# Part of the second layer's weight subtractions on POOL instead of DVE, in a two-layer transformer kernel

## The chip, the cores and the metric

The kernel runs on one core of a Trainium2 chip. The metric is the device time of one execution, from its start to its end, in microseconds (us). A core has five engines that run side by side, each with its own queue of instructions: TensorE (PE) multiplies matrices, VectorE (DVE) and ScalarE (ACT) work on elements, GpSimd (POOL) does too, and SyncE (SP) here issues the loads of weights. Data lie in SBUF; TensorE writes its sums to PSUM.

## The reference

Two layers over 256 tokens of width 1024, in float32. Each adds a mixer and then a mixture of experts to the residual h:

```python
for layer in range(DEPTH):
    u = rms_norm(h, norm_mix[layer])
    mix = even_mixer(...) if layer % 2 == 0 else odd_mixer(...)
    h = h + mix
    h = h + hierarchical_moe(rms_norm(h, norm_ffn[layer]), ...)
```

The change lies in the odd mixer, the second layer's. It projects u to q, k and v, normalises q and k by heads, rotates them by position (rope), and forms attention with the difference of two softmaxes:

```python
q, k, v = jnp.split(u @ w_in, 3, axis=-1)
q = apply_rope(rms_norm(q.reshape(B_, S_, C_HEADS, 2, C_DH), q_norm), positions)
k = apply_rope(rms_norm(k.reshape(B_, S_, C_HEADS, 2, C_DH), k_norm), positions)
...
o = differential_attention(q, k, v, lam, lambda_init, subln)
return o.reshape(B_, S_, ODD_OUT) @ w_out
```

The mixture of experts has a router and 32 experts with a gate, an up and a down matrix each (w_gate, w_up, w_down), whose 2-MB loads are nearly all that the kernel reads.

## The kernel before

The program runs through the layers in order: even mixer, 32 experts, odd mixer, 32 experts. All weights, those of the mixers (w_mix) and of the experts, pass through one ring of buffers in SBUF; SP issues each load (L112) when the slot that it writes is free, so it runs ahead of the computation by as much as the ring holds.

The products of the mixers are made from two parts of each number. A float32 matrix w is split into hi, which TensorE multiplies fast (type fp32r), and lo = w - hi. `mm3` sums three matmuls per product: hi by hi (L291), hi by lo (L292) and lo by hi (L293). The class `Weights` (L295 to L328) makes these splits: a mixer tile of 2 MB comes in four quarters of 128x1024, for each of which ACT casts hi (L314) and DVE subtracts (L315). `ahead` issues splits while split buffers are free (three pairs, `SPLIT`), `next` hands one out and `done` frees it. `W1` is the second layer's instance, with 32 quarters.

The odd mixer has six such projections (`proj_tok`): four for q and k, two for v, then an output projection (`OutProj`). One projection uses four quarters and 48 matmuls of 512 columns, 24 for each half of the tokens (t = 0 and 1). In the first two quarters the halves alternate, in the last two the first half is finished before the second. Below, quarter 0 to 3 belong to projection 1, 4 to 7 to projection 2, and so on; 24 to 31 to the output projection.

Each half of a q or k projection then goes through `rope`: ACT squares it (L374), DVE sums by heads (L376), ACT makes the factor (L245, L246), DVE scales (L379, L381) and multiplies by the cosines (L846) while POOL multiplies by the sines (L847), and DVE joins both (L848, L849). Then TensorE transposes the heads (L388, four instructions), which `settle` puts behind the matmuls of a later projection. Scores and softmax of the heads (L400, L407 and on) are mixed into the following projections. The square and the rope's results use buffers of one small ring ("s2"), in which a new tile waits for the last reader of the old one.

Which instruction stands where on an engine is set by a scheduler that works through the program with its own estimates. Within an engine the order is then fixed, and instructions wait for each other by semaphores.

Of the kernel before, what the change touches and what calls it, by code (L numbers as in the profile page):

```python
# [8 lines left out]
F32 = mybir.dt.float32  # L9
# [4 lines left out]
ALU = mybir.AluOpType  # L14
# [16 lines left out]
SPLIT = 3  # L31
# [93 lines left out]
def halves(t):  # L125
    return t[:, 0:1024], t[:, 1024:2048]
# [13 lines left out]
def hybrid_kernel(ctx: ExitStack, tc: tile.TileContext, x, pos, vec, wr, wbf, const, rope,  # L140
                  w_mix0, w_mix1, w_gate, w_up, w_down, out):
    nc = tc.nc
    V, A, G, T = nc.vector, nc.scalar, nc.gpsimd, nc.tensor
# [151 lines left out]
    class Weights:  # L295


        def __init__(self, n, pairs):
            self.n, self.free, self.used = n, pairs, 0
            self.ready, self.rest = [], []  # L300

        def ahead(self, most=1000):
            while self.n > 0 and most > 0 and (self.rest or self.free > 0):
                most -= 1
                self.n -= 1
                if not self.rest:
                    w = R.take()
                    k = w.shape[1]
                    self.free -= 1
                    self.rest = list(zip([w[:, :, i * P:i * P + P] if k == KD else w[:, i * k // 2:(i + 1) * k // 2, :]  # L310
                                          for i in range(2)], R.alloc(F32R)))
                w, t = self.rest.pop(0)
                hi, lo = (a.rearrange("p (k f) -> p k f", k=w.shape[1]) for a in halves(t))
                self.split = A.copy(out=hi, in_=w)  # L314
                V.tensor_tensor(out=lo, in0=w, in1=hi.bitcast(F32), op=ALU.subtract)  # L315
                if not self.rest:
                    R.drop(1)
                self.ready.append((hi, lo))
# [1029 lines left out]
            with tc.issue_after(silu[0].ins):  # L1348
                A.preload_act_table_set(SET6)

    W1 = Weights(32, SPLIT)
    moe(0, even())
    moe(1, odd(W1))

# [100 lines left out]
```

## Time and profile before

| | us |
|---|---|
| median of 3 runs | 1191.12 |
| lowest, highest | 1190.52, 1192.5 |
| the profiled execution | 1189.17 |
| its span in the trace | 1187.4 |
| TensorE busy | 995.9 (84%) |
| DVE busy | 348.9 (29%) |
| ACT busy | 296.4 (25%) |
| POOL busy | 51.8 (4%) |

The span runs from the first to the last recorded instruction of the profiled execution. Busy shares are means over stages that differ: the experts fill most of the span, and the odd mixer lies between about 603 and 740 us. In that stretch DVE's and POOL's shares are far higher than in the table. In the rows below names such as w, s, o, pa stand for the program's buffers, "out<-in" for what is written and read, and L-numbers for lines of the kernel before; in the changed kernel lines from the changed place on are higher by one (L315 becomes L316, L388 L389).

### The profile page before, as it was taken

The numbers are of one execution on the slowest core, as the hardware profiler recorded it, in microseconds if no ns is written. First come the engines' busy times: TensorE is split into PE (matmuls) and PEld (weight loads), VectorE is DVE, ScalarE is ACT, GpSimd is POOL, SyncE is SP. The second block draws the span as 40 slices with busy tenths as digits, with TensorE's granted clock in tenths as the row PEclk, the third lists the DMA queues.
The fourth block names the chain that finished last, engine by engine and source line by source line (L and its number), as shares of the span: only waits on it lengthen the run. The fifth ranks groups of instructions, "written<-read, shape, count | busy, mean of one in ns | idle before, by whom it ended". The sixth has DMA issues, their size and how long they took to land.

```text
span 1187.4 us, 17231 instructions
## 1 busy us (share of the span) xinstructions
PE 995.9 (84%) x7284; PEld 589.3 (50%) x7284; DVE 348.9 (29%) x879; ACT 296.4 (25%) x681; POOL 51.8 (4%) x90
## 2 busy tenths in 40 slices
PE   7999998888877877786788999888886868786867
PEld 6878774354433434342356778554452424252523
DVE  6976633011111101010069876211111111110101
ACT  6355623111111111111165475211111111111111
POOL 2020001000000000000002100000000000000000
PEclk9999998989979898889899999899899889889989
DMA  9612999999999999999993349899999999999996
GB/s 376 273 54 83 366 374 428 426 427 426 427 427 426 426 427 427 428 427 428 418 428 160 142 166 361 339 427 427 426 427 426 427 427 426 428 427 427 427 427 276
DMA packets 34882, 442.78 MB, mean 373 GB/s; under 512 B 4080, under 2 KB 4464, under 8 KB 7536
## 3 DMA queue, kind: packets, MB, share of 16 engines
q1 hardware_dynamic: 34800, 441.63, 88.7%
q8 instruction: 59, 0.97, 0.3%
q14 instruction: 23, 0.19, 0.0%
HBM read 440.56 MB, written 1.05 MB: 372 GB/s over the span
## 4 chain that ended last, share of the span: by engine, by line
DMA 49%; PE 41%; DVE 5%; ACT 3%; issue 1%; POOL 0%; SPq 0%; ACTq 0%; DVEq 0%; POOLq 0%
DMA w<-w_up 20%; DMA w<-w_down 15%; DMA w<-w_gate 13%; PE pa L1268 7%; PE pa L293 4%; PE pa L291 4%; PE pa L292 4%; PE pa L1277 4%; PE pb L1094 3%; PE pb L1129 2%; PE pc L1243 2%; PE pb L1196 1%; DVE w L315 1%; PE pa L1243 1%; PE pc L400 1%
## 5 line engine op out<-in xcount | busy, mean ns | idle before, releaser
L1268 PE MATMUL pa<-w,o 128*32 128x512 f32 x1920 | 283.0, 683 | 75.8 <-DMA w<-w_up 68.1
L1268 PEld LDWEIGHTS pa<-w,o 128*32 128x32 f32 x1920 | 70.1, 122 | 253.6 <-issue 156.3
L1277 PE MATMUL pa<-w,hid 128*32 128x256 f32 x1984 | 137.7, 424 | 34.6 <-DVE hid L1132 34.6
L1132 DVE TENSOR_TENSOR hid<-hid,pb 128x128 f32<-128x128 f32 x64 | 18.4, 288 | 474.5 <-ACT hid L1131 474.5
L1126 ACT COPY s<-pa 128x512 f32<-128x512 f32 x68 | 39.9, 586 | 398.7 <-PE pa L1268 358.7
L291 PE MATMUL pa<-w 128*128 128x512 f32 (+1 forms) x320 | 120.1, 377 | 3.3 <-ACT w L314 3.3
L292 PE MATMUL pa<-w 128*128 128x512 f32 (+1 forms) x320 | 119.2, 372 | 1.4 <-DVE w L315 1.4
L293 PE MATMUL pa<-w 128*128 128x512 f32 (+1 forms) x320 | 118.8, 373 | 1.8 <-DVE w L315 1.8
L1129 PEld LDWEIGHTS pb<-ct,s 128*128 128x128 f32 x544 | 66.0, 191 | 103.9 <-ACT s L1126 100.3
L1094 PE MATMUL pb<-s,h 128*128 128x128 f32 x448 | 113.7, 407 | 0.0
L1129 PE MATMUL pb<-ct,s 128*128 128x64 f32 (+1 forms) x544 | 74.2, 280 | 45.4 <-ACT s L1126 45.4
L1094 PEld LDWEIGHTS pb<-s,h 128*128 128x128 f32 x448 | 108.9, 334 | 5.8 <-issue 5.8
L1281 DVE COPY o<-pa 32x256 f32<-32x256 f32 x124 | 52.4, 423 | 200.0 <-ACT o L1281 199.4
L1277 PEld LDWEIGHTS pa<-w,hid 128*32 128x32 f32 x1984 | 63.2, 118 | 82.8 <-DVE hid L1132 41.4
L1281 ACT COPY o<-pa 32x256 f32<-32x256 f32 x124 | 45.0, 363 | 207.2 <-PE pa L1277 177.1
L315 DVE TENSOR_TENSOR w<-w 128x1024 fp32r<-128x1024 f32 x68 | 85.1, 1272 | 10.5 <-ACT w L314 10.3
L314 ACT CAST w<-w 128x1024 fp32r<-128x1024 f32 x68 | 68.6, 1045 | 22.5 <-PE pa L293 17.0
L291 PEld LDWEIGHTS pa<-w 128*128 128x128 f32 x320 | 61.8, 193 | 15.4 <-ACT w L314 4.0
L292 PEld LDWEIGHTS pa<-w 128*128 128x128 f32 x320 | 62.1, 194 | 11.8 <-DVE w L315 1.8
L293 PEld LDWEIGHTS pa<-w 128*128 128x128 f32 x320 | 61.9, 194 | 11.5 <-DVE w L315 2.1
L1113 POOL TENSOR_TENSOR s<-OH,CW 128x128 f32<-128x128 f32 x36 | 14.5, 404 | 901.2 <-PE pb L1129 469.3
L1243 PE MATMUL pc<-o,s 128*128 128x512 f32 (+1 forms) x64 | 38.7, 688 | 11.1 <-DVE o L1281 11.1
(284 smaller groups left out, 754.4 us busy)
## 6 DMA issues: line engine op xcount, KB each, us to landing
w<-w_gate SPq DMA_DIRECT2D x62, 2048.0 KB, 39.1
w<-w_up SPq DMA_DIRECT2D x62, 2048.0 KB, 39.1
w<-w_down SPq DMA_DIRECT2D x62, 2048.0 KB, 39.0
w<-w_mix SPq DMA_DIRECT2D x15, 2048.0 KB, 24.4
w<-w_mix SPq DMA_DIRECT2D x4, 1024.0 KB, 9.9
w<-w_gate SPq DMA_DIRECT2D x4, 1024.0 KB, 35.5
w<-w_up SPq DMA_DIRECT2D x4, 1024.0 KB, 30.7
w<-w_down SPq DMA_DIRECT2D x4, 1024.0 KB, 26.2
```

Source lines behind the costliest of these rows:

```text
L291: T.matmul(out=out, lhsT=lhsT[0], rhs=rhs[0], start=start, stop=False)
L292: T.matmul(out=out, lhsT=lhsT[0], rhs=rhs[1], start=False, stop=False)
L293: return T.matmul(out=out, lhsT=lhsT[1], rhs=rhs[0], start=False, stop=stop)
L314: self.split = A.copy(out=hi, in_=w)
L315: V.tensor_tensor(out=lo, in0=w, in1=hi.bitcast(F32), op=ALU.subtract)
L1094: T.matmul(out=pt[:, k, :], lhsT=hk[:, t, 4 * n + k, :], rhs=og[:, t, :], start=t == 0, stop=t == NT - 1)
L1126: A.copy(out=gs, in_=g.rearrange("p (f k) -> p k f", k=4))
L1129: T.matmul(out=tp[:, k, c], lhsT=gs[:, k, :], rhs=r, start=True, stop=True)
L1243: m = T.matmul(out=y[t][:, n, :], lhsT=Sm[:, t * P:(t + 1) * P], rhs=ys, start=start, stop=stop)
L1268: T.matmul(out=gp[32 * j:32 * j + 32, :], lhsT=xg[:, 4 * (j % 2) + kk, 32 * es:32 * es + 32], rhs=w[j][:, kk, :], start=kk == 0, stop=kk = ...
L1277: m = T.matmul(out=dp[32 * j:32 * j + 32, :], lhsT=hid[:, k, :], rhs=w[k // 2][:, k % 2, 256 * j:256 * j + 256], start=k == 0, stop=k == 3 ...
L1281: (V.tensor_copy if j % 2 else A.copy)(out=ys[32 * es:32 * es + 32, 256 * j:256 * j + 256], in_=dp[32 * j:32 * j + 32, :])
```

## The change

`Weights` gets a flag. For the second layer's weights, when the count of quarters still to come is a multiple of four, the subtraction is issued on POOL (`G`) instead of DVE (`V`). These are quarters 3, 7, 11, ... 31: the last of each projection, and the fourth and eighth of the output projection. The first layer's splits stay as they are.

```diff
--- before.py
+++ after.py
@@ -295,8 +295,8 @@
     class Weights:
 
 
-        def __init__(self, n, pairs):
-            self.n, self.free, self.used = n, pairs, 0
+        def __init__(self, n, pairs, shared=False):
+            self.n, self.free, self.used, self.shared = n, pairs, 0, shared
             self.ready, self.rest = [], []
 
         def ahead(self, most=1000):
@@ -312,7 +312,8 @@
                 w, t = self.rest.pop(0)
                 hi, lo = (a.rearrange("p (k f) -> p k f", k=w.shape[1]) for a in halves(t))
                 self.split = A.copy(out=hi, in_=w)
-                V.tensor_tensor(out=lo, in0=w, in1=hi.bitcast(F32), op=ALU.subtract)
+                E = G if self.shared and self.n % 4 == 0 else V
+                E.tensor_tensor(out=lo, in0=w, in1=hi.bitcast(F32), op=ALU.subtract)
                 if not self.rest:
                     R.drop(1)
                 self.ready.append((hi, lo))
@@ -1348,7 +1349,7 @@
             with tc.issue_after(silu[0].ins):
                 A.preload_act_table_set(SET6)
 
-    W1 = Weights(32, SPLIT)
+    W1 = Weights(32, SPLIT, True)
     moe(0, even())
     moe(1, odd(W1))
```

The scheduler places the instructions anew, on TensorE, DVE, ACT and POOL; SP's order is the same. On POOL, in the odd mixer, the kernel before has these rows behind the expert work (s_4184 and s_4200 are the sine products of projection 1, s_4290 and s_4306 of projection 2, s_4396 and s_4412 of projection 3):

```order
L261 TENSOR_TENSOR w<-s_4048,w 128x4x128
L86 MEMSET w 128x1
L847 TENSOR_TENSOR s_4184<-s_4181,own 128x512
L847 TENSOR_TENSOR s_4200<-s_4197,own 128x512
L847 TENSOR_TENSOR s_4290<-s_4287,own 128x512
L86 MEMSET w 128x1
L847 TENSOR_TENSOR s_4306<-s_4303,own 128x512
L847 TENSOR_TENSOR s_4396<-s_4393,own 128x512
L847 TENSOR_TENSOR s_4412<-s_4409,own 128x512
```

And the changed kernel:

```order
L261 TENSOR_TENSOR w<-s_4048,w 128x4x128
L316 TENSOR_TENSOR w<-w 128x1024 x2
L86 MEMSET w 128x1
L848 TENSOR_TENSOR s_4184<-s_4181,own 128x512
L848 TENSOR_TENSOR s_4200<-s_4197,own 128x512
L316 TENSOR_TENSOR w<-w 128x1024 x2
L848 TENSOR_TENSOR s_4290<-s_4287,own 128x512
L86 MEMSET w 128x1
L848 TENSOR_TENSOR s_4306<-s_4303,own 128x512
L316 TENSOR_TENSOR w<-w 128x1024
L848 TENSOR_TENSOR s_4396<-s_4393,own 128x512
```

Quarters 3 and 7 now stand ahead of the first sine product, quarters 11 and 15 between those of projection 1 and projection 2, and quarter 19 ahead of those of projection 3.

On TensorE, around the transposes of projection 1 (s_4181 and s_4197 are its two halves after rope), the kernel before has:

```order
L292 MATMUL pa<-w 128x512
L293 MATMUL pa<-w 128x512
L388 MATMUL pb<-ct,s_4181 128x128 x4
L291 MATMUL pa<-w 128x512
L292 MATMUL pa<-w 128x512
L293 MATMUL pa<-w 128x512
L291 MATMUL pa<-w 128x512
L292 MATMUL pa<-w 128x512
L388 MATMUL pb<-ct,s_4197 128x128 x4
L293 MATMUL pa<-w 128x512
L291 MATMUL pa<-w 128x512
```

And the changed kernel:

```order
L292 MATMUL pa<-w 128x512
L293 MATMUL pa<-w 128x512
L389 MATMUL pb<-ct,s_4181 128x128 x4
L389 MATMUL pb<-ct,s_4197 128x128 x4
L291 MATMUL pa<-w 128x512
L292 MATMUL pa<-w 128x512
L293 MATMUL pa<-w 128x512
L291 MATMUL pa<-w 128x512
L292 MATMUL pa<-w 128x512
L293 MATMUL pa<-w 128x512
```

The second half's transposes have moved ahead of five matmuls, to stand right behind the first half's. It is the same at projection 2, with three matmuls between them before.

On DVE, around the rope of projection 2 (s_4287 and s_4303 are its halves, sm_4281 and sm_4297 the sums of its squares), the kernel before has:

```order
L381 TENSOR_TENSOR s_4287<-pa,sm_4283 128x512
L846 TENSOR_TENSOR s_4289<-s_4287,own 128x512
L315 TENSOR_TENSOR w<-w 128x1024
L848 TENSOR_TENSOR s_4287<-s_4289,s_4290 128x8x32
L849 TENSOR_TENSOR s_4287<-s_4289,s_4290 128x8x32
L376 TENSOR_REDUCE sm_4297<-s_4295 128x8
L315 TENSOR_TENSOR w<-w 128x1024
L379 TENSOR_SCALAR sm_4299<-sm_4299,rsm 128x8
L381 TENSOR_TENSOR s_4303<-pa,sm_4299 128x512
L846 TENSOR_TENSOR s_4305<-s_4303,own 128x512
L848 TENSOR_TENSOR s_4303<-s_4305,s_4306 128x8x32
L849 TENSOR_TENSOR s_4303<-s_4305,s_4306 128x8x32
```

And the changed kernel:

```order
L382 TENSOR_TENSOR s_4287<-pa,sm_4283 128x512
L847 TENSOR_TENSOR s_4289<-s_4287,own 128x512
L849 TENSOR_TENSOR s_4287<-s_4289,s_4290 128x8x32
L850 TENSOR_TENSOR s_4287<-s_4289,s_4290 128x8x32
L377 TENSOR_REDUCE sm_4297<-s_4295 128x8
L316 TENSOR_TENSOR w<-w 128x1024 x2
L380 TENSOR_SCALAR sm_4299<-sm_4299,rsm 128x8
L382 TENSOR_TENSOR s_4303<-pa,sm_4299 128x512
L847 TENSOR_TENSOR s_4305<-s_4303,own 128x512
L849 TENSOR_TENSOR s_4303<-s_4305,s_4306 128x8x32
L850 TENSOR_TENSOR s_4303<-s_4305,s_4306 128x8x32
```

One subtraction has gone from the first half's rope, between L846 (now L847) and L848 (now L849), and two stand now in front of the second half's scaling where one stood.

## Rows read from the trace of the kernel before

**Rows 1.** The page's fourth part, the chain of work that ended last, by engine.

```profile
DMA 49%; PE 41%; DVE 5%; ACT 3%; issue 1%; POOL 0%; SPq 0%; ACTq 0%; DVEq 0%; POOLq 0%
```

**Rows 2.** The view by windows. First the window in us and its length, then the busy time of each engine with its count of instructions, the granted TensorE clock, the mean busy share of the 16 DMA engines, and GB/s.

```profile
605.00:615.00 10.00, 7.66 (x29) 5.63 (x29) 9.66 (x11) 10.00 (x17) 2.52 (x2) 0.83 1.01 425
...
625.00:635.00 10.00, 9.50 (x44) 7.53 (x43) 9.23 (x12) 5.99 (x9) 3.55 (x2) 1.00 0.92 390
635.00:645.00 10.00, 9.17 (x43) 7.67 (x44) 9.96 (x15) 5.15 (x9) 1.75 (x2) 1.00 0.06 26
645.00:655.00 10.00, 7.79 (x34) 5.08 (x33) 7.99 (x13) 4.93 (x10) 2.67 (x2) 0.83 0.13 25
...
725.00:735.00 10.00, 10.00 (x53) 8.36 (x51) 5.12 (x7) 3.36 (x8) 0.00 (x0) 1.00 0.93 387
...
745.00:760.00 15.00, 13.34 (x99) 9.41 (x102) 2.91 (x12) 4.50 (x11) 0.00 (x0) 0.87 0.65 247
760.00:1000.00 240.00, 198.13 (x1552) 103.14 (x1548) 35.80 (x107) 33.04 (x83) 4.88 (x12) 0.92 1.01 427
```

**Rows 3.** The timeline of SP's queue, which issues the weight loads: start, length, line and operation.

```profile
737.43 0.38 SPq L112 DMA_DIRECT2D w<-w_up  x1
754.30 0.33 SPq L112 DMA_DIRECT2D w<-w_down  x1
```

**Rows 4.** The list of waits from 604 to 660 us, all engines: who waits for whom, us in total, times, longest.

```profile
PE pb L388 <- DVE s L849: 3.5, 2, 2.2
...
DVE s L848 <- POOL s L847: 2.3, 3, 1.2
```

**Rows 5.** The timeline of TensorE (PE) in the same stretch: start, length, line and operation, and in brackets the idle time before it and what ended it.

```profile
617.11 0.38 PE L822 MATMUL pb<-sm,ct 64*128 64x2 f32 x2
...
635.83 0.66 PE L388 MATMUL pb<-ct,s 128*128 128x128 f32 x4 [1.33 <-DVE s L849]
...
637.94 0.39 PE L291 MATMUL pa<-w 128*128 128x512 f32 x1
...
645.87 0.40 PE L293 MATMUL pa<-w 128*128 128x512 f32 x1
...
649.62 0.63 PE L388 MATMUL pb<-ct,s 128*128 128x128 f32 x4 [2.21 <-DVE s L849]
...
650.87 0.79 PE L291 MATMUL pa<-w 128*128 128x512 f32 x1
651.46 0.63 PE L292 MATMUL pa<-w 128*128 128x512 f32 x1
...
653.96 0.40 PE L292 MATMUL pa<-w 128*128 128x512 f32 x1
```

**Rows 6.** The groups of instructions by line from 600 to 756 us: count, busy time, mean ns of one, idle time before.

```profile
L315 DVE TENSOR_TENSOR w<-w 128x1024 fp32r<-128x1024 f32 x32 | 41.7, 1314 | 5.1 <-ACT w L314 5.0
```

**Rows 7.** The timeline of DVE, columns as in rows 5; xN folds N instructions in a row.

```profile
610.25 5.75 DVE L315 TENSOR_TENSOR w<-w 128x1024 fp32r<-128x1024 f32 x5
...
616.00 0.14 DVE L820 TENSOR_TENSOR sm<-vt 64x2 f32<-64x2 f32 x1
...
624.30 0.22 DVE L379 TENSOR_SCALAR sm<-sm,rsm 128x8 f32<-128x8 f32 x1
624.43 1.22 DVE L315 TENSOR_TENSOR w<-w 128x1024 fp32r<-128x1024 f32 x1
...
632.78 2.33 DVE L315 TENSOR_TENSOR w<-w 128x1024 fp32r<-128x1024 f32 x1
...
635.36 0.41 DVE L849 TENSOR_TENSOR s<-s,s 128x256 f32<-128x256 f32 x1
...
641.15 2.32 DVE L315 TENSOR_TENSOR w<-w 128x1024 fp32r<-128x1024 f32 x1
...
649.05 0.42 DVE L849 TENSOR_TENSOR s<-s,s 128x256 f32<-128x256 f32 x1
...
654.58 0.68 DVE L376 TENSOR_REDUCE sm<-s 128x8 f32<-128x512 f32 x1
...
657.80 1.68 DVE L846 TENSOR_TENSOR s<-s,own 128x512 f32<-128x512 f32 x1
```

**Rows 8.** POOL's groups by line and shape over the whole span, columns as in rows 6.

```profile
L1113 POOL TENSOR_TENSOR s<-OH,CW 128x128 f32<-128x128 f32 x36 | 14.5, 404 | 901.2 <-PE pb L1129 469.3 <-DVE CW L1035 179.2 <-issue 135.3
...
L261 POOL TENSOR_TENSOR w<-s,w 128x512 fp32r<-128x512 f32 x4 | 5.1, 1276 | 56.0 <-ACT w L261 56.0
```

**Rows 9.** The timeline of POOL, columns as in rows 5.

```profile
626.39 1.81 POOL L847 TENSOR_TENSOR s<-s,own 128x512 f32<-128x512 f32 x1 [6.31 <-DVE s L381]
632.28 1.74 POOL L847 TENSOR_TENSOR s<-s,own 128x512 f32<-128x512 f32 x1 [4.08 <-DVE s L381]
640.68 1.71 POOL L847 TENSOR_TENSOR s<-s,own 128x512 f32<-128x512 f32 x1 [6.66 <-DVE s L381]
...
654.11 1.70 POOL L847 TENSOR_TENSOR s<-s,own 128x512 f32<-128x512 f32 x1 [5.43 <-DVE s L381]
657.62 1.31 POOL L847 TENSOR_TENSOR s<-s,own 128x512 f32<-128x512 f32 x1 [1.82 <-DVE s L381]
...
678.13 1.28 POOL L847 TENSOR_TENSOR s<-s,own 128x512 f32<-128x512 f32 x1 [2.87 <-DVE s L381]
```

## The prediction

> **What bounds the kernel now.** I read the page first. Its chain of waits is DMA and TensorE by turns, with 5% of it on DVE [rows 1]: whether DVE's subtractions matter must be read from their own stretch. The view by windows shows where that is. From 760 us on the DMA engines are full (share 1.01, 427 GB/s), so the second layer's experts run at the speed of their weights. Of the windows between 605 and 655 us, in the second layer's mixer, four have TensorE at 7.66 to 9.50 of 10 us; DVE is at 9.66 and 9.96 in two of them, and the granted clock at 0.83 in two; by 725 to 735 TensorE is 10.00 of 10 [rows 2]. So the mixer's first half is where DVE holds TensorE, and its second half is bound by TensorE itself.
>
> Does a delay in the mixer reach the end? SP's queue issues an expert's w_up at 737.43 and can issue the next load only at 754.30, when L1216 frees its slot [rows 3]; in 745 to 760 the DMA share is 0.65, about 5 us of idle transfer time [rows 2]. The ring of weights is full by then, so a microsecond lost or won by the mixer moves L1216, the next transfers, and the end by one (a gain by at most those 5 us). I take the factor 1.
>
> What DVE makes TensorE wait for is the rope: the wait list has L388, the transposes of rotated heads, 3.5 us behind DVE's L849 in two waits, and DVE's L848 2.3 us behind POOL's L847 [rows 4]. The two waits are 1.33 and 2.21 us [rows 5]. After the second the matmuls L291 and L292 last 0.79 and 0.63 us, at 653.96 again 0.40: the granted clock is at its lower level (1.2 instead of 2.4 GHz) in between. The work of these 4.34 us (649.62 to 653.96) would take about 2.7 at the usual spacing, so I count 1.6 us for it. The usual spacing is 7.93/35 = 0.227 us a matmul (36 rows from 637.94 to 645.87).
>
> **What one moved subtraction costs.** On DVE the 32 subtractions take 41.7 us, 1314 ns on average [rows 6]; undisturbed it is 1.22 (624.43), spaced by 1.15 where five stand in a row (5.75/5) [rows 7]. POOL does none before, so I bound it. Its two-operand 128x512 takes 1276 ns (L261, fp32r output as here) and 1.28 to 1.31 in the undisturbed L847, its 128x128 404 ns [rows 8, 9]. The slope (1276-404)/384 = 2.27 ns a column gives 1276 + 512x2.27 = 2.44 us for 1024 columns; twice 1.31 is 2.62; if it waits as the slowest L847 does, twice 1.81 is 3.6. I take 2.5 as an estimate, since L261 is nearest.
>
> A page puts it lower: the Trainium skill, "GPSIMD Engine Reference", section 3.1, gives 4497 ns for a two-operand addition of 2048 fp32 elements against 2293 on DVE; half of that is an estimate of 2.25 us, and four subtractions on the path at 0.25 less would bring the sum below to about 1197.5. No run here shows POOL at that length.
>
> Does it run beside DVE? The rows say no, where DVE reads two SBUF operands. L315 at 632.78 takes 2.33 instead of 1.22, and POOL's L847 stands at 632.28 to 634.02; at 641.15 it takes 2.32 against POOL's 640.68 to 642.39; L846 at 657.80 takes 1.68 instead of 0.69 against 657.62 to 658.93 [rows 7, 9]. In each case the DVE instruction ends its normal length after POOL ends. L376 at 654.58 (one operand) lies under POOL's 654.11 to 655.81 and takes its 0.68 [rows 7, 9]. So they take turns by whole instructions, and whichever asks while the other runs is next. A moved subtraction frees 1.15 to 1.22 us of DVE and shuts out every two-operand DVE instruction for 2.5.
>
> The Trainium skill, "SBUF — State Buffer", section "Who interferes with whom", has the same rule: a DVE instruction with two SBUF inputs contends with a GpSimd instruction that reads SBUF, and the holder keeps the shared pair for its whole instruction. The trace agrees (2.33 against 1.22). By the rule the change gives the pair 2.5 us of work for 1.2; without it DVE would simply be 1.2 us shorter, which is the first rival below.
>
> **Part by part.** Eight quarters of 32 go to POOL (3, 7, 11, ... 31). The scheduler also moves their neighbours on TensorE, DVE and ACT; SP keeps its order. I walked the new order with the durations above, from the same state at 610 us. The casts (ACT) and loads stay the same; POOL itself is idle there, so its own 20 us (8x2.5) cost nothing but the port and what is queued behind.
>
> Quarter 3: POOL holds the port about 611.4 to 613.9, where DVE had a run of five subtractions from 610.25 [rows 7]. The small operations behind (L820 at 616.00) end at 617.5, and L822's matmul, now after 25 projection matmuls instead of 29 (at 617.11 before [rows 5]), waits 1.4 us. That uses up most of what the lost subtraction saves DVE.
>
> Quarters 7 and 11, projection 1: the first rope half is ready 1.4 earlier. POOL then has quarter 11 right behind the second half's product, and DVE has quarter 10 between; POOL asks while DVE subtracts, so it is next for 2.5, and L848 and L849 end at about 636.5, not 635.77 (635.36+0.41 [rows 7]). The transposes of both halves now stand together, so 5 matmuls that used the wait before come behind it: 0.7 + 5x0.227 = 1.9 us late.
>
> Quarter 15, projection 2: it stands on POOL in front of the first half's product. From the end of one rope (635.77) to the end of the second half of the next (649.05+0.42 = 649.47 [rows 7]) before took 13.7 us. Now: +0.7 late start, +1.4 since ACT's square waits for the slot that the late rope frees, +2.5 for quarter 15 ahead of the product, -1.15 for its place on DVE, +1.15 since two subtractions instead of one stand in front of the second half: 4.6, that is 654.1. Three matmuls that stood between the halves' transposes come behind (0.7): TensorE is 5.3 late there. This includes the 1.9. Its wait grows from 2.21 to about 5.7.
>
> Quarter 19, projection 3: it shuts out that projection's rope and DVE's work on the first scores. My walk has TensorE wait 2.6 there if the port goes to POOL each time, 1.0 if the score work gets in first: I take the middle, 1.8. Quarter 23: between 0 and 1.0, I take 0.4 (DVE is less full by then). Quarters 27 and 31, of the output projection: TensorE is 10.00 of 10 at 725 to 735 and DVE 5.12 [rows 2], so this slack covers 2.5 us each; without that cover it would be up to 1.3 (2.5-1.2) each.
>
> Sum: 5.3+1.8+0.4 = +7.5. The profiled execution took 1189.17 us (span 1187.4): 1196.7; the median of the runs is 1.95 higher (1191.12), so the forecast is 1198.6, say 1198.5. A second fall of the clock would add 1.6, a port that DVE wins at quarters 15 and 19 would take off about 3.5: its own range is 1194 to 1202.
>
> **Rivals.** *Faster: DVE is relieved.* In 635 to 645 DVE is busy 9.96 of 10, and its L849 is what TensorE waits for. If POOL finds the port while DVE works on PSUM or one-operand instructions, two subtractions less before the second rope of projection 2 (2x1.2 = 2.4) cover its wait of 2.21, one less covers 1.33, and the slow clock's 1.6 goes too: -5.1, 1186.0. It decides if the rope of projection 2 ends before TensorE comes to its transposes, about 646.5. Against it: the free stretches there are of 0.2 to 0.7 us (L376 0.68, L379 0.22), and POOL wants 2.5. Chance 0.17.
>
> *No difference.* The waits change places (1.4 at L822 for 1.33 at L388, quarter 15 within the existing 2.21) and the sum of the TensorE waits stays. It needs quarter 15 not to come ahead of the product. 1191, within 2.4 either way. Chance 0.13.
>
> *Worse than forecast.* No slack anywhere in six projections: 8x(2.5-1.2) = 10.4 and two more falls of the clock at 1.6: +13.6, 1204.7. For it: ropes or scores are tied to DVE in all projections. Against it: full TensorE by 655 to 735. Chance 0.13.
>
> That the change does not do what it says is excluded by the order of the new kernel: eight subtractions stand on POOL.
>
> The Trainium skill, "Perfetto Trace Analysis", section "Optimizing Scalar/DVE Operations", warns that moving work between GPSIMD and DVE might not help since they share a read port. It speaks for the forecast's side, by the rows on L315 above.
>
> **How the numbers follow.** The forecast has 0.57. A measurement of this kernel can tell 0.2%, 2.4 us, from no change. Slower by more than that: 0.57+0.13 = 0.70; same 0.13; faster 0.17. The 80% range leaves out half of the faster case below and a little of the worst above: 1188 to 1204.5.
>
> **What would show it.** Right: eight POOL subtractions of 2.4 to 2.6 us where nobody disturbs them; DVE's two-operand rows of 2.5 to 3.7 us under them; a wait of L389 (the old L388) behind L850 that grows from 2.21 to 5 or 6 us; TensorE at 10 of 10 after 680, and 745 to 760 as before but later by the same amount as the end. Wrong: a POOL row below 1.9 us; DVE rows at 1.2 under POOL's; L389 without waits; or an end that moves less than L1216 does.

## The result and the profile after

The changed kernel takes 1201.37 us, median of 4 runs (1200.39 to 1203.02), against 1190.82 of the kernel before in runs on the same chip (1190.31 to 1192.5): 10.55 us slower, ratio 1.0088 with a 95% interval of 1.007 to 1.0105. The profiled execution took 1203.02 us (span 1201.4), so it stands 1.65 above its median, as that of before stood about as much below. The spans differ by 14.0 us; 1.13 of that lies ahead of the odd mixer, whose first projection matmul starts at 608.17 instead of 607.04. Times below are compared after taking off these 1.13.

The chain that ended last, by engine (the page's fourth part), where [rows 1] stood before, and POOL's new group from the groups by line and shape:

```profile
DMA 51%; PE 35%; DVE 7%; ACT 4%; issue 2%; POOL 0%; SPq 0%; ACTq 0%; DVEq 0%; POOLq 0%
```

```profile
L316 POOL TENSOR_TENSOR w<-w 128x1024 fp32r<-128x1024 f32 x8 | 20.5, 2565 | 81.2 <-ACT w L314 69.7 <-DVE w L316 6.7 <-ACT sm L246 4.8
```

TensorE's share has fallen from 41% to 35% and DVE's has risen from 5% to 7%, though DVE does eight instructions less. A subtraction on POOL takes 2565 ns on average.

The view by windows, columns as in [rows 2]:

```profile
605.00:615.00 10.00, 7.15 (x29) 5.08 (x28) 9.66 (x10) 9.04 (x14) 5.27 (x3) 0.83 1.02 430
...
635.00:645.00 10.00, 8.71 (x43) 7.16 (x42) 8.87 (x9) 6.32 (x10) 3.45 (x2) 1.00 0.12 51
645.00:655.00 10.00, 4.66 (x25) 3.81 (x23) 6.68 (x12) 3.30 (x6) 3.64 (x4) 0.82 0.00 0
655.00:665.00 10.00, 10.00 (x35) 6.81 (x33) 8.10 (x13) 4.13 (x9) 4.20 (x3) 0.67 0.37 118
...
735.00:745.00 10.00, 10.00 (x46) 8.28 (x46) 5.54 (x6) 3.23 (x6) 2.39 (x1) 1.00 0.77 297
...
755.00:765.00 10.00, 8.60 (x35) 8.49 (x36) 3.05 (x15) 0.00 (x0) 0.00 (x0) 0.61 0.82 347
...
772.00:1000.00 228.00, 185.09 (x1479) 94.12 (x1479) 33.83 (x104) 33.66 (x85) 4.92 (x12) 0.93 1.01 427
```

In the mixer's first half TensorE is now at 4.66 of 10 us in 645 to 655, where it had 7.79 [rows 2], and the granted clock is low in two windows in a row (0.82 and 0.67). From 735 to 745 TensorE and the clock are full again. The clock falls once more at 755 to 765, in the router, to 0.61. From 772 on the DMA engines are full, as before.

POOL's timeline, where [rows 9] stood:

```profile
612.09 2.76 POOL L316 TENSOR_TENSOR w<-w 128x1024 fp32r<-128x1024 f32 x1 [2.92 <-ACT w L314]
621.57 2.40 POOL L316 TENSOR_TENSOR w<-w 128x1024 fp32r<-128x1024 f32 x1 [6.72 <-DVE w L316]
...
632.87 3.34 POOL L316 TENSOR_TENSOR w<-w 128x1024 fp32r<-128x1024 f32 x1
642.76 2.39 POOL L316 TENSOR_TENSOR w<-w 128x1024 fp32r<-128x1024 f32 x1 [6.55 <-ACT w L314]
645.11 1.75 POOL L848 TENSOR_TENSOR s<-s,own 128x512 f32<-128x512 f32 x1
...
658.07 2.35 POOL L316 TENSOR_TENSOR w<-w 128x1024 fp32r<-128x1024 f32 x1 [4.77 <-ACT sm L246]
...
737.58 2.39 POOL L316 TENSOR_TENSOR w<-w 128x1024 fp32r<-128x1024 f32 x1 [13.54 <-ACT w L314]
```

Undisturbed the subtraction takes 2.35 to 2.40 (658.07, 621.57). The 3.34 at 632.87 begin while DVE still subtracts. At 642.76 quarter 15 stands right in front of the sine product of projection 2 (L848, 645.11).

DVE's timeline, where [rows 7] stood:

```profile
611.38 6.82 DVE L316 TENSOR_TENSOR w<-w 128x1024 fp32r<-128x1024 f32 x4
...
618.19 0.14 DVE L821 TENSOR_TENSOR sm<-vt 64x2 f32<-64x2 f32 x1
...
633.91 2.59 DVE L849 TENSOR_TENSOR s<-s,s 128x256 f32<-128x256 f32 x1
636.42 0.41 DVE L850 TENSOR_TENSOR s<-s,s 128x256 f32<-128x256 f32 x1
...
642.88 2.82 DVE L847 TENSOR_TENSOR s<-s,own 128x512 f32<-128x512 f32 x1
646.89 0.43 DVE L849 TENSOR_TENSOR s<-s,s 128x256 f32<-128x256 f32 x1 [1.19 <-POOL w L86]
...
653.67 0.42 DVE L850 TENSOR_TENSOR s<-s,s 128x256 f32<-128x256 f32 x1
...
658.08 2.37 DVE L380 TENSOR_SCALAR sm<-sm,rsm 128x8 f32<-128x8 f32 x1 [0.99 <-ACT sm L246]
```

L849 at 633.91 takes 2.59 instead of 0.41, and L847 at 642.88 takes 2.82 instead of 0.69: both end behind POOL's subtraction by 0.29 and 0.55, a little less than their own length. The row at 658.08 was not expected: L380 reads 8 columns and a scalar per partition, takes 0.22 elsewhere [rows 7], and here 2.37, under POOL's 658.07 to 660.42.

TensorE's timeline, where [rows 5] stood, and one row of ACT's:

```profile
608.17 0.73 PE L291 MATMUL pa<-w 128*128 128x512 f32 x2 [0.94 <-ACT w L314]
...
618.48 0.35 PE L823 MATMUL pb<-sm,ct 64*128 64x2 f32 x2 [1.08 <-DVE sm L821]
...
636.89 0.66 PE L389 MATMUL pb<-ct,s 128*128 128x128 f32 x4 [1.29 <-DVE s L850]
...
654.24 1.08 PE L389 MATMUL pb<-ct,s 128*128 128x128 f32 x4 [5.34 <-DVE s L850]
...
661.44 0.48 PE L291 MATMUL pa<-w 128*128 128x512 f32 x1
```

```profile
636.95 0.69 ACT L375 ACTIVATE s<-pa,rsm 128x512 f32<-128x512 f32 x1 [5.20 <-DVE s L850]
```

TensorE's waits are 1.08 at L823, 1.29 at projection 1's second transposes and 5.34 at projection 2's (before: none, 1.33 and 2.21). After the last the matmuls are slow until 661.44. ACT's row is the square of projection 2's first half: it waits 5.20 for DVE's L850, the end of projection 1's rope.

SP's queue, where [rows 3] stood:

```profile
750.00 0.39 SPq L112 DMA_DIRECT2D w<-w_up  x1
768.38 0.33 SPq L112 DMA_DIRECT2D w<-w_down  x1
```

The load of w_down is issued at 768.38 instead of 754.30.

How late TensorE is at the same projection matmul shows where the time goes. The matmuls (L291 to L293) are counted from the mixer's first, which is number 0, and timed from its start; each value is a kernel's timeline against that of the kernel before, in us. Where other instructions were placed on the other side of a matmul, a value swings by one or two us.

| matmul number | 48 | 120 | 168 | 192 | 360 |
|---|---|---|---|---|---|
| changed kernel | 1.1 | 1.1 | 6.0 | 6.8 | 11.5 |
| f1, subtractions on POOL, old order | 0.2 | 2.6 | 0.2 | 1.7 | 1.7 |
| f2, subtractions on DVE, new order | 0.0 | -1.5 | 2.3 | 2.6 | 5.5 |
| h2, new order, quarter 15 on POOL | 0.1 | -1.5 | 1.5 | 3.2 | 6.1 |
| h4, new order, quarters 3, 7, 11 on POOL | 1.1 | 1.1 | 5.3 | 5.6 | 8.5 |
| e5, old subtractions, sine products on DVE | -0.2 | -1.6 | -5.4 | -6.8 | -6.5 |

The letters are those of the experiments below. The kernel before ran about 1.6 us under its median in its profile, so most of these rows lie about 1 us above the differences of the medians.

### The profile page after: what moved, and what is told of

The parts are those of the page before. It is cut to its first block, busy times and chain, and to the rows that moved or that the text cites. A ratio compares the mean times of both kernels' runs of the same rounds, so it can differ in the third digit from the quotient of the medians.

```text
span 1201.4 us, 17244 instructions
## 1 busy us (share of the span) xinstructions
PE 1001.4 (83%) x7284; PEld 590.9 (49%) x7284; DVE 356.1 (30%) x871; ACT 295.5 (25%) x681; POOL 72.0 (6%) x98
## 4 chain that ended last, share of the span: by engine, by line
DMA 51%; PE 35%; DVE 7%; ACT 4%; issue 2%; POOL 0%; SPq 0%; ACTq 0%; DVEq 0%; POOLq 0%
DMA w<-w_up 22%; DMA w<-w_down 15%; DMA w<-w_gate 13%; PE pa L1269 6%; PE pa L291 4%; PE pa L293 4%; PE pa L292 4%; PE pa L1278 3%; PE pb L1095 3%; DVE w L316 2%; PE pb L1130 2%; PE pb L1197 1%; PE pc L1244 1%; PE pa L1244 1%; PE pc L401 1%
## 5 line engine op out<-in xcount | busy, mean ns | idle before, releaser
L1278 PE MATMUL pa<-w,hid 128*32 128x256 f32 x1984 | 140.4, 431 | 34.6 <-DVE hid L1133 34.6
L291 PE MATMUL pa<-w 128*128 128x512 f32 (+1 forms) x320 | 120.8, 379 | 3.3 <-ACT w L314 3.3
L293 PE MATMUL pa<-w 128*128 128x512 f32 (+1 forms) x320 | 118.9, 373 | 2.2 <-DVE w L316 2.2
L316 DVE TENSOR_TENSOR w<-w 128x1024 fp32r<-128x1024 f32 x60 | 79.3, 1344 | 7.7 <-ACT w L314 7.6
L291 PEld LDWEIGHTS pa<-w 128*128 128x128 f32 x320 | 62.3, 195 | 14.7 <-ACT w L314 3.9
L293 PEld LDWEIGHTS pa<-w 128*128 128x128 f32 x320 | 62.3, 195 | 12.7 <-DVE w L316 2.4
```

The costliest lines, as they stand in the source:

```text
L291: T.matmul(out=out, lhsT=lhsT[0], rhs=rhs[0], start=start, stop=False)
L293: return T.matmul(out=out, lhsT=lhsT[1], rhs=rhs[0], start=False, stop=stop)
L316: E.tensor_tensor(out=lo, in0=w, in1=hi.bitcast(F32), op=ALU.subtract)
L1278: m = T.matmul(out=dp[32 * j:32 * j + 32, :], lhsT=hid[:, k, :], rhs=w[k // 2][:, k % 2, 256 * j:256 * j + 256], start=k == 0, stop=k == 3 ...
```

## Experiments

Times are medians; the difference is to the median of the kernel before in the runs that go with it (1190.4 to 1191.1). Where two changed kernels are compared below, their medians are subtracted; by the differences of the table the result would shift by up to 0.4.

| run | us | difference | ratio, 95% interval |
|---|---|---|---|
| e1_q15 | 1191.21 | +0.8 | 0.9994 to 1.0016 |
| e2_all_but_q15 | 1198.91 | +8.5 | 1.0058 to 1.0084 |
| e3_out_proj | 1191.24 | +0.8 | 0.9995 to 1.0012 |
| e4_sines_on_dve | 1193.35 | +2.9 | 1.0014 to 1.0036 |
| f1_pool_old_order | 1191.39 | +0.6 | 0.9998 to 1.0016 |
| f2_dve_new_order | 1195.35 | +4.6 | 1.0025 to 1.0054 |
| e5_no_pool | 1182.14 | -8.7 | 0.9917 to 0.9943 |
| g4_old_act_order | 1202.01 | +10.9 | 1.0076 to 1.0105 |
| g2_pool_no_sines | 1195.15 | +4.1 | 1.002 to 1.0044 |
| h2_q15_new_order | 1195.63 | +4.8 | 1.0029 to 1.0057 |
| h3_sines_back_on_pool | 1185.6 | -5.3 | 0.994 to 0.9967 |
| h4_first_three | 1199.17 | +8.5 | 1.0056 to 1.0082 |

**Which quarter.** Three kernels change the condition in `Weights.ahead`; in each the scheduler places everything anew.

```diff
-                E = G if self.shared and self.n % 4 == 0 else V
+                E = G if self.shared and self.n == 16 else V
```

> Only quarter 15 (the one that stands on POOL ahead of projection 2's first sine product) goes to POOL. Theory 'place' (what a moved subtraction costs depends on what it stands in front of; in the changed kernel's trace TensorE's delay grows by 4.6 us at projection 2): the wait of L389 at projection 2 is 4 to 6 us instead of 2.2, the end 4 to 5 us later than before, about 1195. Theory 'amount' (each of the eight costs the same, 10.5/8 = 1.3): about 1192. Theory 'order' (the scheduler's joined transposes cost, not POOL): the three matmuls behind them cost 0.7, about 1191.5.

Measured: +0.8, no difference that can be told. "Place" falls in this form. But the order has changed as well: the subtraction now runs before the first half of projection 2 is scaled, and not right in front of its sine product.

```diff
+                E = G if self.shared and self.n % 4 == 0 and self.n != 16 else V
```

> Seven quarters on POOL, quarter 15 back on DVE; the transposes of projections 1 and 2 still stand joined. 'Place': the end about 4.6 us earlier than the changed kernel's 1201.4, about 1196.5 to 1197. 'Amount': 7 x 1.3 = 9.2 over before, about 1200. 'Order': as the changed kernel, 1201.

Measured: +8.5, between the theories (2.5 less than the changed kernel, by the differences 2.1). Most of the change's cost is there without quarter 15.

```diff
+                E = G if self.shared and self.n in (4, 0) else V
```

> Only quarters 27 and 31, of the output projection, go to POOL, where TensorE was at 10 of 10 before and DVE at 5 of 10 us. 'Place': no difference, 1191 within 1. 'Amount': 2 x 1.3 = 2.6 later, about 1193.5.

Measured: +0.8, no difference that can be told, as "place" had it: in this kernel, where TensorE is full and DVE half idle, the two subtractions on POOL cost nothing that can be told.

**The sine products on DVE, in the changed kernel.**

```diff
-            G.tensor_tensor(out=b.rearrange("p n a d -> p n (a d)"), in0=qn, in1=sgt, op=ALU.mult)
+            V.tensor_tensor(out=b.rearrange("p n a d -> p n (a d)"), in0=qn, in1=sgt, op=ALU.mult)
```

> The changed kernel with the rope's sine product (L848) on DVE as well, so that POOL has only the eight subtractions. If the harm is that subtractions stand ahead of the sine products in POOL's queue: most of the 4.6 us of projection 2 comes back, about 1196. If the harm is that POOL's subtraction shuts DVE out for 2.5 us wherever it stands: DVE also gets 8 x 0.69 us more, no gain, 1200 to 1203.

Measured: +2.9, so 7.6 of the 10.5 come back, more than the queue theory wanted. It could be the queue, the port, or another order of the scheduler: this run alone does not tell.

**Order or engine.** The scheduler's order can be held. After the program is traced, edges without a wait are added between successive instructions of an engine, in the order of a table that is taken from another kernel:

```python
...
for text in ORDER:
    n, last = 0, None
    for step in text.split():
        n += int(step)
        i = at["I-%d" % n]
        if last is not None:
            tc.add_manual_dep(i, last.name, mybir.DependencyInfo(
                mybir.DependencyClass.NoSync, mybir.DependencyReason.DATA), reason="fixed_order")
        last = i
...
```

`at` finds an instruction of the mixer by its name, which is the same in all these kernels; a table covers TensorE, DVE and ACT in the odd mixer. Rows that a kernel has on another engine are left out of the table. POOL's order, and in f2 the places of the eight subtractions on DVE, are still the scheduler's. In f1 the changed kernel gets the old order, in f2 the kernel before gets the new one.

> All eight subtractions on POOL as in the changed kernel, but TensorE, DVE and ACT are held to the order of the kernel before (the eight rows left out of DVE's); POOL has quarter 15 ahead of projection 2's first sine product and quarter 11 ahead of projection 1's second. Theory 'engine' (POOL's 2.5 us on the shared port and in front of the sine products cost the time): 1198 to 1202, the wait of L389 at projection 2 stays at 5 us. Theory 'order' (the scheduler's new order costs it): 1191 to 1193. Both in part: 1194 to 1197.

> All subtractions on DVE as before, but TensorE, DVE and ACT are held to the changed kernel's order, with the eight subtractions put between where the scheduler finds them ready. 'Engine': 1191 to 1193. 'Order': 1198 to 1202, with the later projections' delays (3 us between matmuls 208 and 250, 2 between 300 and 350) as in the changed kernel. Both in part: 1194 to 1197.

Measured: f1 +0.6, no difference that can be told; f2 +4.6. So neither theory holds alone. With the old order the eight moved subtractions cost nothing that can be told; the new order costs 4.6 with no subtraction moved; both together cost 10.55, so some 5.4 come only from the two together (10.55 - 0.6 - 4.6); the intervals of these differences are 1 to 2 us to either side.

f2's wait for the ropes, from TensorE's timeline, and its windows:

```profile
649.83 0.63 PE L426 MATMUL pb<-ct,s 128*128 128x128 f32 x4 [4.33 <-DVE s L887]
```

```profile
645.00:655.00 10.00, 5.40 (x22) 3.06 (x21) 6.71 (x11) 4.41 (x8) 1.77 (x1) 0.77 0.00 0
655.00:665.00 10.00, 10.00 (x39) 7.22 (x39) 9.13 (x21) 3.77 (x10) 3.07 (x2) 0.89 0.57 210
```

Before, the two rope waits were 1.33 and 2.21 [rows 5]. In f2 they are one of 4.33, since the first pair of transposes now finds its data ready, and the clock is low in both of its windows (before, 0.83 and 1.00). By matmul 168 that is 2.3 us; another 2.9 are lost between matmuls 192 and 360, where f2 has no subtraction on POOL either.

f1's waits in TensorE's timeline (its lines are higher by 38: L427 is the transposes of L389), and two rows of POOL's (L354 is a subtraction, L886 a sine product):

```profile
637.55 1.11 PE L427 MATMUL pb<-ct,s 128*128 128x128 f32 x4 [2.25 <-DVE s L888]
...
651.93 0.63 PE L427 MATMUL pb<-ct,s 128*128 128x128 f32 x4 [1.36 <-DVE s L888]
```

```profile
638.16 2.70 POOL L354 TENSOR_TENSOR w<-w 128x1024 fp32r<-128x1024 f32 x1 [2.42 <-ACT w L352]
642.98 1.72 POOL L886 TENSOR_TENSOR s<-s,own 128x512 f32<-128x512 f32 x1 [2.12 <-DVE s L420]
```

Here quarter 15 is subtracted from 638.16 to 640.86, and the sine product waits for DVE at 642.98: the subtraction has gone where POOL was idle. The waits are 2.25 and 1.36, 3.61 in sum, against 3.54 before.

**POOL out of the ropes, subtractions as before.** The edit is that of e4, made in the kernel before.

> The kernel before with the rope's sine product (L847) on DVE too, so that POOL does nothing in projections 1 to 4. If the exclusion of whole instructions is what the trace shows, L847 on POOL holds DVE up by 1.1 to 1.2 us each time (2.33 instead of 1.22) and takes 0.69 on DVE: 0.4 to 0.5 us gained per half in projections 1 and 2, the waits of L388 1.33 and 2.21 become shorter by about 1 each, 1188 to 1190. If POOL's work were really beside DVE's, 8 x 0.69 us more on DVE: 1193 to 1196.

Measured: -8.7, more than expected. Windows, and two rows of DVE's timeline (L847 is the sine product):

```profile
625.00:635.00 10.00, 10.00 (x49) 8.12 (x48) 9.86 (x16) 6.73 (x10) 0.00 (x0) 1.00 0.86 365
635.00:645.00 10.00, 10.00 (x47) 8.27 (x46) 9.90 (x16) 5.51 (x10) 0.10 (x1) 1.00 0.04 18
645.00:655.00 10.00, 10.00 (x52) 7.11 (x50) 9.85 (x25) 6.39 (x14) 0.00 (x0) 1.00 0.44 156
```

```profile
626.14 0.69 DVE L847 TENSOR_TENSOR s<-s,own 128x512 f32<-128x512 f32 x1
...
632.34 1.22 DVE L315 TENSOR_TENSOR w<-w 128x1024 fp32r<-128x1024 f32 x1
```

TensorE is at 10.00 of 10 in the three windows where it had 9.50, 9.17 and 7.79 [rows 2], and the clock does not fall. The sine product takes 0.69 on DVE, and the subtraction behind it 1.22 instead of 2.33 [rows 7]. This kernel beats both.

> The kernel without POOL in the ropes (e5, 1182.1) with TensorE, DVE and ACT held to its order, and the eight sine products back on POOL. If e5's gain of 8.7 us is that DVE is no longer shut out and no longer waits for the products: 1189 to 1194. If it is its order: 1182 to 1184.

Measured: h3 has e5's order, with the sine products back on POOL: 1185.6, -5.3. So of e5's 8.7 some 5 come from its order and 3.5 (1185.6 - 1182.1) from the engine. Both expectations missed; the parts lie side by side.

> The kernel with the sine products on DVE (1182.1), with TensorE, DVE and ACT held to its own order, and the eight subtractions moved to POOL. There DVE is busy 9.8 to 9.9 of 10 us from 625 to 655 and TensorE never waits for a rope. If a moved subtraction costs DVE more than it frees (2.5 against 1.2 us, five of them in projections 1 to 4): 1185 to 1190. If only the order had made the change slow: 1181 to 1183.

Measured: 1195.15, 13.0 above e5 with e5's order: beyond the range that was written down. DVE's timeline (L419 is the old L379, L355 a subtraction, L888 the old L848):

```profile
630.25 2.37 DVE L419 TENSOR_SCALAR sm<-sm,rsm 128x8 f32<-128x8 f32 x1
...
638.13 3.01 DVE L355 TENSOR_TENSOR w<-w 128x1024 fp32r<-128x1024 f32 x1
...
650.12 2.59 DVE L888 TENSOR_TENSOR s<-s,s 128x256 f32<-128x256 f32 x1
```

Three times in projections 1 to 3 a row of DVE takes 1.8 to 2.2 us more than alone (0.22, 1.22, 0.42), in a stretch in which DVE has no idle time to give. By matmul 168 TensorE is 5.8 later than in e5 (0.4 against -5.4). A fourth such row comes under quarter 23, and by matmul 240 TensorE is another 5 us later:

```profile
669.41 2.37 DVE L450 TENSOR_SCALAR sm<-sm 128x4 f32<-128x4 f32 x1
```

Alone this row takes 0.16. So the same eight subtractions cost 13 us here, 6 in the changed kernel's order and 0.6 in the old order.

**ACT's order alone.** The table holds ACT only, to the old order.

> The changed kernel with ACT alone held to the order of the kernel before, where the casts of quarters 12 to 14 stand ahead of the square of projection 2's first half (L374, L375 in the changed kernel); TensorE, DVE and POOL are placed by the scheduler around it, with both transposes still joined. Theory 'casts behind the square' (ACT waits 5.2 us for the slot of the square with four casts queued behind it, so quarter 15's subtraction comes to POOL just as the sine product does): 1192 to 1195, ACT's wait in front of the square under 1 us. Theory 'joined transposes and DVE's order': 1198 to 1201.

Measured: 1202.0, no better than the changed kernel and above both ranges. ACT no longer waits in front of the square, as that theory wanted, but the time is not shorter: the theory of the casts falls in this form. The scheduler answered with another order on DVE, whose timeline has three subtractions in a row (L337) ahead of the sum that projection 2's first half needs:

```profile
638.49 5.67 DVE L337 TENSOR_TENSOR w<-w 128x1024 fp32r<-128x1024 f32 x3
```

**Within the new order: which subtractions.** Tables as in f2, some of the subtractions on POOL.

> TensorE, DVE and ACT held to the changed kernel's order as in f2, with quarter 15 alone on POOL, ahead of projection 2's first sine product, and the other seven subtractions on DVE. In f2 (all on DVE) 1195.4, in the changed kernel (all eight on POOL, same order) 1201.4. Theory 'place': quarter 15 makes half of these 6.0 (rope of projection 2 ends 3.6 us later in the changed kernel's trace than in f2's), 1198 to 1199.5. 'Amount': an eighth, 1196.

Measured: 1195.63, 0.3 over f2, so "place" falls again; "amount" (1196) is near. TensorE's timeline:

```profile
650.38 1.09 PE L427 MATMUL pb<-ct,s 128*128 128x128 f32 x4 [5.39 <-DVE s L888]
```

The wait is 5.39 instead of f2's 4.33, and rope and transposes are 1.1 later there. But the granted clock comes back sooner than in f2 (0.77 and 0.89 in these windows):

```profile
645.00:655.00 10.00, 4.62 (x18) 3.06 (x19) 6.74 (x10) 4.42 (x8) 1.77 (x1) 0.83 0.00 0
655.00:665.00 10.00, 8.75 (x38) 6.18 (x37) 9.27 (x23) 3.23 (x7) 3.05 (x2) 1.00 0.56 210
```

So at matmul 168 h2 is even 0.8 ahead of f2. By matmul 360 it is 0.6 behind, and 0.3 in the median, within the uncertainty of both. So the rope does come later with quarter 15 on POOL, and in the profiled execution the clock gave most of it back. With seven other quarters on POOL, quarter 15 is worth 2.1 to 2.5 (e2 against the changed kernel; TensorE's order is the same in both, DVE's and ACT's differ in two rows each).

> TensorE, DVE and ACT held to the changed kernel's order, with quarters 3, 7 and 11 (the ones ahead of and inside projection 1's rope) on POOL and the other five on DVE. The traces have projection 1's second rope half 3.0 us later after its start in the changed kernel than in f2, before quarter 15 comes. Theory 'carry' (that delay passes on through ACT's square, which waits for this rope, to projection 2 and TensorE): at least half of the 6.0 between f2 (1195.4) and the changed kernel, 1198 to 1200. Theory 'amount': three eighths of it, 1197.5; if it is absorbed like quarter 15 alone (h2): 1195 to 1196.

Measured: 1199.17, 3.8 over f2, of the 6.0 that the changed kernel is over it. "Carry" holds. TensorE's and ACT's timelines (L861 is L823, L427 is L389, L413 is L375):

```profile
616.52 0.35 PE L861 MATMUL pb<-sm,ct 64*128 64x2 f32 x2 [1.15 <-DVE sm L859]
...
634.94 0.66 PE L427 MATMUL pb<-ct,s 128*128 128x128 f32 x4 [1.31 <-DVE s L888]
...
651.20 1.09 PE L427 MATMUL pb<-ct,s 128*128 128x128 f32 x4 [4.23 <-DVE s L888]
```

```profile
635.00 0.69 ACT L413 ACTIVATE s<-pa,rsm 128x512 f32<-128x512 f32 x1 [5.21 <-DVE s L888]
```

Two of the three waits are the changed kernel's (1.15 and 1.31, there 1.08 and 1.29) and ACT's square waits 5.21 (there 5.20) for the end of projection 1's rope: the delay is handed to projection 2 before quarter 15 is subtracted at all. By the table TensorE is 2.6 later than in f2 already at matmul 120 (1.1 against -1.5), by the first two waits, and 3.0 at 168. What the hand-over does is that f2's long wait does not swallow these 2.6: the rope of projection 2 comes later by as much, and the wait stays at 4.23 (f2 4.33). The other five quarters add the last 2.2 us.

## Why the prediction was right, and where not

- **Sign and size.** Slower by 7.5 was forecast, 10.55 came; the median lies in the range of 1188 to 1204.5, but not far from the end of the forecast's own range (1202). That it lies there is in part luck: 4.6 of the 10.55 are the new order's without POOL, and some terms of the sum were too large where others were too small.
- **A subtraction's time.** 2.5 was taken, 2.35 to 2.40 measured undisturbed, 2.565 on average. The estimate from L261 was near. Half of the 4497 ns for 2048 elements in the Trainium skill, "GPSIMD Engine Reference", section 3.1, is an estimate of 2.25; the trace stands between the two.
- **The port.** Right for two-operand rows (L847 2.82, L849 2.59). Left out was that L380, with one operand and a scalar, is shut out too (2.37 for 0.22); the forecast had counted L379, its line before, among the stretches that are free for POOL. The Trainium skill, "SBUF — State Buffer", section "Who interferes with whom", does name tensor_scalar among the operations that can take the shared pair; the trace agrees.
- **Quarter 3.** 1.4 of wait at L823 predicted, 1.08 measured, and nothing of it is made good.
- **Quarter 11.** The port changed hands as predicted, but the rope ended at 636.83 - 1.13 = 635.70, not 636.5, so TensorE was 1.1 late at matmul 120, not 1.9.
- **Projection 2.** 5.3 late predicted, a wait of 5.7; 6.0 and 5.34 measured. The sum was near; its terms were not. The rope ended at 654.09 - 1.13 = 652.96 (654.1 predicted), 3.5 later than before instead of 4.6. With the 0.7 of the three matmuls that makes 4.2 of the 6.0; the other 1.8 were lost at the lower clock, which lasted until 661.44 after the wait (before, until 653.96) and stood in the forecast's range, not in its sum. The forecast charged 2.5 to quarter 15; h2 shows that it alone, in this order, makes the rope 1.1 later and the kernel 0.3 slower. The first three quarters cost 3.8 in that order (h4), since ACT's square hands their delay on. That hand-over was in the sum with 1.4.
- **Quarter 19.** 1.8 predicted, 0.8 measured (6.0 to 6.8).
- **From quarter 23 on.** This step failed: "Quarter 23: between 0 and 1.0, I take 0.4", with slack for 27 and 31. TensorE loses 4.7 us there (6.8 to 11.5), and from 680 to 690 it is busy 8.55 of 10 us, where the forecast's signs wanted 10 of 10 after 680. What was missed is, first, that the scheduler's new order loses time in these projections by itself: f2 loses 2.9 there without POOL, and h4, with these quarters on DVE, 2.9 too. The other 1.8 come with the later quarters on POOL: beside f2, the changed kernel falls back by 1.0 between matmuls 204 and 228, where quarter 23 is subtracted, and by 0.8 between 300 and 324, behind quarter 27. The slack for 27 and 31 is real only in e3's order (no difference). In the list of waits from 662 to 742 us the weight loads of the scores wait more for DVE in the changed kernel and in f2 than before, here the changed kernel, f2 and the kernel before:

```profile
PEld pc L401 <- DVE sm L408: 3.3, 5, 0.9
```

```profile
PEld pc L438 <- DVE sm L445: 1.9, 3, 1.0
```

```profile
PEld pc L400 <- DVE sm L407: 0.9, 2, 0.6
```

- **The factor 1.** Right. TensorE's lateness of 11.5 at the mixer's end and the 1.13 ahead of it make 12.6; SP's load is 14.1 later, as the router also runs at a lower clock (0.61 in 755 to 765; the kernel before has 0.84 in the same stretch, 742.4 to 752.4), and the span is 14.0 longer. The bound of 5 us on a gain was wrong: e5 gains 8.7, and TensorE's lead of 6.5 at matmul 360 is more than 5 already.
- **The rivals.** *Faster* needed POOL to find the port free. f1 shows that this can happen (quarter 15 is subtracted where POOL was idle), though with no gain: the rope waits stay 3.6 in sum. The forecast took the new order as given and, but for the matmuls behind the joined transposes, put its cost on POOL; the runs put 4.6 on the order alone.

Open is why the new order loses its 2.9 us in the later projections, row by row, and which of its moves does it; the longer waits of the weight loads were found there, but no run removes them. Joined transposes stand in f2 with one wait of 4.33 instead of two, but they were not tried apart from the rest.

## What to carry to other kernels

When a scheduler places the work, moving one instruction to another engine is two changes: the engine and a new order everywhere. Hold the order, and try each alone, before giving a result to the engine; here the order alone cost 4.6 us, the engine 0.6, 6 or 13 by the order it met. POOL was no spare DVE here for operations on two operands in SBUF: taking POOL's eight sine products off it gained 8.7 us, 3.5 of them by the engine.

## What the hardware showed that was not expected

A DVE instruction on 8 columns with a scalar operand (L380) waits for POOL's whole subtraction: 2.37 us against 0.22, again 2.37 at 630.25 in g2, so it is not only long two-operand instructions that lose. The scalar need not come from SBUF: L450 in g2 multiplies 4 columns by a constant and takes 2.37 instead of 0.16 under POOL. The sum over 512 columns (L376, 0.68 under POOL [rows 7]) does not.

How long the lower clock lasts does not follow from the length of the wait in front of it. After f2's wait of 4.33 the granted clock is 0.77 and 0.89 in two windows; after h2's of 5.39, with TensorE in the same order, it is 0.83 and 1.00 in the same two. The kernel before, with waits of 1.33 and 2.21, has 0.83 and 1.00. These are one profile each.
